# One-core hybrid attention layer: six gates into the seven-product pairs, two key sets as separate heads, named attention buffers, softmax scaling on two engines

## The chip, the cores and the metric

One core of one Trainium2 chip runs the whole layer. The metric is the device time of one execution in microseconds (us). The core's engines are TensorE (PE in the profile; PEld is its weight load), VectorE (DVE), ScalarE (ACT), GpSimd (POOL) and SyncE (SP), whose queue issues most of the transfers.

## What is computed

One decoder layer over 1024 tokens of width 1024, fp32 in and out: a norm, one wide projection, three attention mixers, a gated merge, an output projection, and a gated FFN with a short convolution.

```python
proj = h @ w_in[l] + b_in[l]
(qa, ka, va, fa, qb, kb, vb, qc, kc_, vc_, ksl, vsl, kwn, vwn, gc, gates) = jnp.split(proj, split_at, axis=-1)
y_a = fox_attention(qa, ka, va, fa)             # 4 heads, causal, decay = cumsum(log_sigmoid(fa))
y_b = dilated_attention(qb, kb, vb, dil_slopes) # 6 heads, windows 128/512/2048 at strides 1/4/16
y_c = nsa_attention(qc, kc_, vc_, ksl, vsl, kwn, vwn, gc, nsa_slopes, ...)  # 6 heads
#   per head:  o = gb[..., 0:1] * o_c + gb[..., 1:2] * o_s + gb[..., 2:3] * o_w
#   o_c: compressed keys, o_s: selected blocks of 64 keys, o_w: the last 512 keys
g = jax.nn.sigmoid(gates).reshape(B_, S, 3, D)
merged = (g[:, :, 0] * (y_a @ w_pa[l]) + g[:, :, 1] * (y_b @ w_pb[l])
          + g[:, :, 2] * (y_c @ w_pc[l]))
x = x + merged @ w_o[l]
x = x + conv_ffn(rms_norm(x, norm2_g[l]), w_up[l], conv_w[l], conv_b[l], w_down[l])
```

The 3072 columns of `gates` are 24 tiles of 128 features; a "gate" below is one of these tiles for all 1024 tokens.

## The kernel before

Every fp32 operand is split into a high and a low part (`hTh`, `hTl`; `wh`, `wl`), and a product takes three matmuls (`mm3`, L273 to L275). A 128-column weight tile against 1024 tokens is 8 x 2 x 3 = 48 matmuls of 128x512 (`dense`). In `proj_pairs` two weight tiles are taken together by a seven-product scheme (Strassen): 7 x 4 x 3 = 84 matmuls of 128x512 instead of 96, paid for with sums of weight tiles (L562 to L571) and of token tiles (`token_sums`, L461 to L474) on POOL, DVE and ACT and with adds of the products on DVE (L596, L597).

The stages, in us from the start of the span: norm and transposes to 57; `fox_decay` (L711 to L727, a chain over DVE, ACT and two small matmuls L721, L722), gates 0 and 1 (`gate`, evacuated by DVE at L1400, stored from ACT's queue at L1403), the token sums and eight tiles of `proj_vn` (L662, L694) to about 115; nine pairs to 297; key and value compression (`compress_in`, `compress`) with gate 2 to 348; attention to 832; the gates left over, and `branch`, to about 902; `merge` to 985; output projection, FFN and the last norm to 1758.

In attention the order of PE, DVE and ACT is written out beforehand by a planner, `Flow`: processes ask for an engine with a level and a cost, or for a place in a ring (`S` 2, `T` 2, `PV` 1, `dn` 1, `p` 4, `th` 3), and the lowest level that is ready goes first. One unit is two blocks of 128 queries of a head. `strips` makes the scores (L787, L790, L791); `soften` takes the maximum (L814), the exponential with its sum (ACT, L822), then on DVE the floor and reciprocal of the sum (L833, L834) and the multiply of the row (L836, or L838 where the NSA gate is a second factor); `turner` transposes blocks into one bank (L881); `splitter` makes the high part on ACT (`th`, L897) and the low part on DVE (`tl`, L900); `products` sums into the one `PV` bank (L927, L928); `pv_out` copies on ACT (L943), adds on DVE (L947) and stores 64 KB (L952) from a ring of four `yt` tiles that the planner does not know of. There are 64 units: an NSA unit holds compressed, selected and local keys in one `PV` sum. Where PE has nothing else, `fill` gives it the matmuls of gates 3 and up (L1428), evacuated by ACT (L1439) from the one `dn` bank and stored by SP (L1442).

Behind attention `gate` finishes the gates that `fill` has not reached, while `branch` loads eight 512 KB tiles of the mixers' outputs (L1477), casts them (ACT, L1478) and subtracts (DVE, L1479). `merge` needs all of `y_a`, then `y_b`, then `y_c`.

## Time and profile before

| | |
|---|---|
| median of 3 runs | 1759.94 us (1757.18 to 1762.91) |
| the profiled execution, its own time | 1759.76 us |
| span of its trace | 1758.0 us |
| TensorE busy in the span | 1676.7 us, 95% |
| VectorE, ScalarE, GpSimd busy | 74%, 44%, 27% |

The span runs from the first to the last instruction of the trace; 1.76 us lie around it. Busy shares are means over stages with different limits, so the stretches of single stages matter more than the table. "Granted clock" is the share of full speed that TensorE was given. A wait is put down to the engine and line that came last.

### The profile page before, as it was taken

What the parts mean: (1) busy time and instruction counts of PE and PEld (TensorE: products, weight loads), DVE (VectorE), ACT (ScalarE), POOL (GpSimd) and SP (SyncE); (2) the same over time, 40 slices, a digit from 0 to 9 for tenths busy, and PEclk for the clock granted to TensorE, in tenths of its full rate; (3) what the DMA queues carried; (4) which work ended last, traced back from release to release, by engine and by line L of the source; (5) the groups of instructions that cost most, each with busy time, mean ns of one, the idle gap of its engine ahead of it and who ended that gap; (6) DMA issues with size and microseconds to landing.
All of it is one profiled execution on the core that took longest, in us unless ns stands there. A gap on an engine that the chain in (4) does not pass through costs nothing.

```text
span 1758.0 us, 24330 instructions
## 1 busy us (share of the span) xinstructions
PE 1676.7 (95%) x8504; PEld 1383.7 (79%) x8504; DVE 1301.9 (74%) x2189; ACT 777.6 (44%) x1493; POOL 465.9 (27%) x326
## 2 busy tenths in 40 slices
PE   6889999899999999999999999899999999999998
PEld 6688888678787877787787788688888878888876
DVE  8856676567886888787227616999999999866764
ACT  5323443356454655565425413433333334354452
POOL 3652322100101000100214320655456554200000
PEclk9989999999999999999999999999999999999999
DMA  6445566867786235311625630144545445487661
GB/s 203 127 117 144 156 168 171 200 171 193 202 222 177 53 85 161 95 34 34 216 96 196 209 131 13 31 162 144 191 156 192 168 154 163 135 265 235 209 227 55
DMA packets 224321, 266.49 MB, mean 152 GB/s; under 512 B 20712, under 2 KB 160078, under 8 KB 223990
## 3 DMA queue, kind: packets, MB, share of 16 engines
q1 hardware_dynamic: 219862, 254.81, 48.6%
q10 hardware_dynamic: 3888, 7.34, 1.2%
q0 software_dynamic: 448, 2.78, 0.6%
q8 instruction: 67, 1.10, 0.3%
q14 instruction: 56, 0.46, 0.1%
HBM read 187.23 MB, written 80.36 MB: 152 GB/s over the span
## 4 chain that ended last, share of the span: by engine, by line
PE 57%; DVE 21%; issue 7%; DMA 5%; ACT 5%; POOL 3%; SPq 0%; POOLq 0%; DVEq 0%; ACTq 0%
PE dn L1428 8%; PE dn L273 5%; PE dn L274 5%; PE dn L275 5%; PE S L275 3%; PE S L274 3%; PE T L881 3%; PE S L273 3%; DVE t L1690 3%; DVE u L1748 3%; PE PV L928 2%; PE T L275 2%; PE T L273 2%; PE T L274 2%; PE S L791 2%
## 5 line engine op out<-in xcount | busy, mean ns | idle before, releaser
L897 ACT CAST th<-T 128x512 fp32r<-128x512 f32 (+2 forms) x202 | 100.4, 507 | 92.3 <-PE T L881 88.2
L1456 POOL TENSOR_TENSOR wl<-wr,wh 128x1024 fp32r<-128x1024 f32 x15 | 35.8, 2387 | 392.3 <-ACT wh L1452 285.7
L900 DVE TENSOR_TENSOR tl<-T,th 128x512 fp32r<-128x512 f32 (+2 forms) x202 | 115.3, 586 | 28.5 <-ACT th L897 27.2
L814 DVE TENSOR_REDUCE sm<-S 128x1 f32<-128x640 f32 (+7 forms) x128 | 88.1, 713 | 38.2 <-PE S L791 37.6
L1428 PE MATMUL dn<-hTh,wh 128*128 128x512 f32 x240 | 101.7, 424 | 10.7 <-ACT f L1439 8.1
L1690 DVE SCALAR_TENSOR_TENSOR t<-u,ccols,t 128x511 f32<-128x511 f32 (+1 forms) x88 | 95.7, 1088 | 7.5 <-ACT t L1685 6.4
L927 PE MATMUL PV<-th,v 128*128 128x256 f32 (+1 forms) x362 | 94.1, 280 | 6.6 <-DVE yt L947 5.8
L1428 PE MATMUL dn<-hTh,wl 128*128 128x512 f32 x240 | 99.7, 415 | 0.0
L1428 PE MATMUL dn<-hTl,wh 128*128 128x512 f32 x240 | 99.1, 413 | 0.0
L881 PE MATMUL T<-ident,p 128*128 128x128 f32 x610 | 97.9, 277 | 0.2 <-DVE p L838 0.2
L822 ACT ACTIVATE p<-S,sm 128x640 f32<-128x640 f32 (+7 forms) x128 | 90.9, 715 | 15.1 <-DVE sm L814 13.2
L928 PE MATMUL PV<-tl,v 128*128 128x256 f32 (+1 forms) x362 | 91.3, 286 | 4.8 <-DVE tl L900 4.6
L791 PE MATMUL S<-k,q 114*128 114x512 f32 (+6 forms) x240 | 90.1, 384 | 0.0
L251 POOL TENSOR_TENSOR wl<-wr,wh 128x384 fp32r<-128x384 f32 (+2 forms) x35 | 51.8, 1480 | 135.7 <-ACT wh L249 126.0
L787 PE MATMUL S<-k,q 128*128 128x512 f32 (+3 forms) x240 | 81.7, 340 | 1.9 <-ACT p L822 1.8
L273 PE MATMUL dn<-hTh,wh 128*128 128x512 f32 x204 | 81.1, 397 | 1.2 <-ACT f L1439 0.8
L274 PE MATMUL dn<-hTl,wh 128*128 128x512 f32 x204 | 80.7, 395 | 0.0
L928 PEld LDWEIGHTS PV<-tl,v 128*128 128x128 f32 x362 | 69.3, 191 | 12.9 <-DVE tl L900 8.2
L927 PEld LDWEIGHTS PV<-th,v 128*128 128x128 f32 x362 | 69.3, 191 | 11.8 <-DVE yt L947 7.8
L881 PEld LDWEIGHTS T<-ident,p 128*128 128x128 f32 x610 | 70.7, 141 | 5.8 <-DVE tl L900 1.2
L1615 POOL TENSOR_TENSOR su<-wr 128x512 f32<-128x512 f32 x20 | 31.6, 1579 | 143.2 <-DMA wr<-w_up 84.6
L275 PE MATMUL dn<-hTh,wl 128*128 128x512 f32 x176 | 69.4, 395 | 0.0
(784 smaller groups left out, 5377.5 us busy)
## 6 DMA issues: line engine op xcount, KB each, us to landing
wr<-w_up SPq DMA_DIRECT2D x66, 256.0 KB
wr<-w_in SPq DMA_DIRECT2D x26, 512.0 KB
gr<-dg SPq DMA_DIRECT2D x24, 512.0 KB
t<-w_down SPq DMA_DIRECT2D x22, 512.0 KB
dt<-t SPq DMA_DIRECT2D x22, 512.0 KB
wr<-dl SPq DMA_DIRECT2D x39, 256.0 KB
x<-x SPq DMA_DIRECT2D x16, 512.0 KB
dg<-f SPq DMA_DIRECT2D x30, 256.0 KB
```

The lines of the kernel that those rows point to most:

```text
L273: nc.tensor.matmul(out, st[0], mv[0], start=first, stop=False)
L274: nc.tensor.matmul(out, st[0], mv[1], start=False, stop=False)
L275: nc.tensor.matmul(out, st[1], mv[0], start=False, stop=last)
L791: nc.tensor.matmul(out, q.t[1][0:R, qs], k.t[1][0:R, cs], start=False, stop=True)
L822: nc.scalar.activation(o.rearrange("p a b -> p (a b)"), u, AF.Exp, bias=mx[:, x:x + 1], accum_out=sm[:, 2 + x:3 + x])
L881: nc.tensor.transpose(ps[:, n * P:(n + 1) * P], b(), self.ident)
L897: nc.scalar.copy(g.th[:, cs], ps[:, cs])
L900: yield "DVE", 0, 0.07 + cs.stop * 1.04e-3, lambda: nc.vector.tensor_tensor(g.tl[:, cs], ps[:, cs], g.th[:, cs].bitcast(F32), ALU.subtract)
L927: nc.tensor.matmul(unit.pv[:, oc], w, g.th[:, cs], start=first and i == 0, stop=False)
L928: nc.tensor.matmul(unit.pv[:, oc], w, g.tl[:, cs], start=False, stop=e)
L1428: nc.tensor.matmul(p, w[i][:, k], self.hT[hh][j][:, k], start=x == 0, stop=x == 23)
L1690: nc.vector.scalar_tensor_tensor(o, i, cw[2 - sh], o, ALU.mult, ALU.add)
```

## The change

- `PAIRED = 18`: gates 18 to 23 leave `fill` and `gate` and become three more pairs of `proj_pairs` (252 matmuls of 128x512 for 288). Their tiles go to `dg` from the pairs' own buffers by SP.
- The selected (`n`) and local (`w`) keys of an NSA head become separate heads: 88 units for 64, each with its own `PV` sum, copy, add and store. `dy_c` gets two planes, and `branch` loads both and adds them (L1514 to L1517): 11 loads of 512 KB instead of 8.
- Attention buffers get names that the planner hands out: PSUM `S0`, `S1`, `PV`, and `X0` to `X2` shared by transposes and `fill`; SBUF `p0` to `p5`, four `th`/`tl`, eight `y`. The planner now counts the stores and loads (`move`).
- `soften` makes the two factors on DVE (`factors`, 128x2, the NSA gates multiplied in), and each row's multiply is offered to DVE (L864) and ACT (L865); in the planned order 104 of 176 stand on DVE and 72 on ACT, these 72 with 34,432 of the 78,080 columns.
- Gates 0 and 1 are evacuated by ACT, gate 2 by DVE, and `fox_decay` moves behind `proj_vn`.

```diff
+    PAIRED = 18
+        gate = lambda f: (C_G + f * P, 20 + f, lambda side: lambda hh, src: nc.sync.dma_start(
+            self.dg[f][:, hh * 512:hh * 512 + 512], src))
-                 (k("s", C_KSL, 18, 0), k("w", C_KWN, 19, 0)))
+                 (k("s", C_KSL, 18, 0), k("w", C_KWN, 19, 0)),
+                 *((gate(f), gate(f + 1)) for f in range(self.PAIRED, 24, 2)))
...
-        self.S, self.T, self.PV, self.dn = (Ring(self, n) for n in (2, 2, 1, 1))
-        self.p, self.th, self.ce = (Ring(self, n) for n in (4, 3, 2))
+        self.S, self.PV = r("S0", "S1"), r("PV")
+        self.T = self.dn = r("X0", "X1", "X2")
+        self.p, self.th, self.y, self.ce = r(*(f"p{i}" for i in range(6))), r(*range(4)), r(*(f"y{i}" for i in range(8))), r(0, 1)
...
+        def factors():
+            nc.vector.tensor_scalar(ls, sm[:, 2:4], TINY, None, ALU.max)
+            nc.vector.reciprocal(sm[:, 6:8], ls)
+            if pair.gates is not None:
+                nc.vector.tensor_tensor(sm[:, 6:8], sm[:, 6:8], pair.gates, ALU.mult)
...
+    def norm(self, pair, x, left):
+        nc, F = self.nc, self.F
+        p, f, n = pair.blocks[x], pair.sm[:, 6 + x:7 + x], (pair.rows[x][2] - pair.rows[x][1] + 1) * P
+        yield [("DVE", 1, 0.13 + n * 0.47e-3, lambda: nc.vector.tensor_scalar(p, p, f, None, ALU.mult)),
+               ("ACT", 3, 0.16 + n * 0.85e-3, lambda: nc.scalar.mul(p, p, f))]
...
     def pv_out(self, unit):
+        place = yield F.y
...
-            if f > 2:
+            if f != 2:
                 nc.scalar.activation(gt[:, cs], ps, AF.Identity, bias=self.cols[:, 20 + f:21 + f])
+                self.step(2)
             else:
-                out = nc.vector.tensor_scalar(gt[:, cs], ps, self.cols[:, 20 + f:21 + f], None, ALU.add)
-                with self.tc.issue_after(out.ins):
-                    self.step(2)
+                nc.vector.tensor_scalar(gt[:, cs], ps, self.cols[:, 20 + f:21 + f], None, ALU.add)
...
-        for f in range(3, 21):
+        for f in range(3, self.PAIRED):
...
-            raw = pool.tile([P, S], F32, "gr")
-            nc.sync.dma_start(raw, dy[k])
+            raw, *more = (self.st.tile([P, S], F32, "gr") for _ in range(dy[k].shape[0]))
+            nc.sync.dma_start(raw, dy[k][0])
+            for x in more:
+                nc.sync.dma_start(x, dy[k][1])
+                nc.vector.tensor_tensor(raw, raw, x, ALU.add)
...
         self.proj_va()
-        self.fox_decay()
         self.gate(0)
...
         self.proj_vn(vn)
+        self.fox_decay()
...
-        self.ap2 = Pool(self, "att2", {"p": 4, "pc": 2})
+    ORDER = (("f", 0), ("d", 0), ("d", 1), ("f", 1), ("d", 2), ("d", 3), ("s", 0), ("f", 2), ("d", 4), ("d", 5),
+             ("s", 1), ("f", 3), ("w", 0), ("w", 1), ("w", 2), ("n", 0), ("n", 1), ("n", 2), ("w", 3), ("w", 4), ("w", 5),
+             ("n", 3), ("n", 4), ("n", 5))
```

The order of ACT in the early part, before: the exponential and logarithm of `fox_decay` (`fax`, `flf`, L713 and L714) stand among the casts of `proj_vn`'s weights (`bh`) and of the token sums (`T1h`).

```order
L638 CAST bh_168_814<-wr_171_821 128x548
L461 CAST T1h_120_470<-f4_148_689 128x512
L713 ACT_TABLE_LOAD
L713 ACTIVATE fax_151_698<-fax_151_698 128x32
L714 ACT_TABLE_LOAD
L714 ACTIVATE flf_152_699<-fax_151_698,cm_150_696 128x32
L638 CAST bh_168_814<-wr_172_826 128x548
L638 CAST bh_168_814<-wr_173_831 128x548
```

And in the change (L731 and L732 are `fox_decay`, L1436 is the evacuation of gate 0, `f4`):

```order
L656 CAST bh_161_786<-wr_165_798 128x548
L1436 ACTIVATE f4_150_696<-dn_157_709,cols_95_364 128x512
L656 CAST bh_161_786<-wr_166_803 128x548
L473 CAST T2h_122_472<-f4_148_689 128x512
L1440 DMA dg_60_165<-f4_150_696 128x512
L473 CAST T2h_122_472<-sh_159_774 128x512
L731 ACT_TABLE_LOAD
L731 ACTIVATE fax_204_1176<-fax_204_1176 128x32
L473 CAST T3h_124_474<-sl_160_775 128x512
L732 ACT_TABLE_LOAD
L732 ACTIVATE flf_205_1177<-fax_204_1176,cm_203_1174 128x32
```

`fox_decay` has gone behind the second half of the token sums, and ACT has the gates' evacuations between its casts.

The order of ACT in the middle of attention, before: casts `th`, exponentials (L822) and the copies of finished units.

```order
L943 COPY yt_1345_7083<-PV_1334_7026 64x256
L822 ACTIVATE p_1347_7094,sm_1336_7043<-S_1337_7044,sm_1336_7043 128x640
L897 CAST th_1348_7097<-T_1344_7078 128x512
L897 CAST th_1352_7109<-T_1350_7100 128x384
L822 ACTIVATE p_1356_7123,sm_1336_7043<-S_1346_7088,sm_1336_7043 128x768
L822 ACTIVATE p_1358_7146,sm_1354_7112<-S_1355_7113,sm_1354_7112 128x640
```

And in the change, at the like place (L841 exponential, L865 multiply of a row, L970 copy, L923 cast `th`):

```order
L923 CAST th1_1251_6813<-X2_1247_6793 128x256
L923 CAST th2_1253_6823<-X0_1250_6809 128x384
L841 ACTIVATE p3_1256_6833,sm_1243_6781<-S0_1244_6782,sm_1243_6781 128x640
L865 ACTIVATE p4_1248_6796<-p4_1248_6796,sm_1237_6751 128x384
L970 COPY y7_1259_6852<-PV_1249_6803 64x256
L841 ACTIVATE p2_1261_6860,sm_1243_6781<-S1_1255_6826,sm_1243_6781 128x640
L923 CAST th0_1264_6874<-X2_1260_6854 128x512
L970 COPY y0_1267_6887<-PV_1262_6864 64x256
```

ACT's queue has a new kind of instruction in it, the multiply L865, with an exponential before it and a copy, an exponential and a cast behind.

The order of SP's queue behind attention, before: the last gate tiles stored by `fill` (L1442), then the loads of `branch` (L1477) and of `merge` (L1489).

```order
L1442 DMA dg_60_165<-f4_1795_9118 128x512
L1477 DMA gr_1799_9161<-dy_a0_49_154 128x1024
L1477 DMA gr_1800_9165<-dy_a1_50_155 128x1024
L1477 DMA gr_1803_9171<-dy_b0_51_156 128x1024
L1442 DMA dg_60_165<-f4_1795_9118 128x512
L1477 DMA gr_1804_9175<-dy_b1_52_157 128x1024
L234 DMA wr_1814_9202<-w_in 128x8x128
L1477 DMA gr_1805_9179<-dy_b2_53_158 128x1024
L1477 DMA gr_1808_9185<-dy_c0_54_159 128x1024
L1477 DMA gr_1809_9189<-dy_c1_55_160 128x1024
L1477 DMA gr_1810_9193<-dy_c2_56_161 128x1024
L1489 DMA gr_1852_9572<-dg_60_165 128x1024
```

And in the change (L1479 gates, L1514 and L1516 the two planes, L1529 `merge`'s gate tiles):

```order
L1479 DMA dg_60_165<-f4_1896_9597 128x512 x2
L246 DMA wr_1936_9838<-w_pb 128x3x128
L1514 DMA gr_1900_9641<-dy_a0_49_154 128x1024
L1514 DMA gr_1901_9645<-dy_a1_50_155 128x1024
L1514 DMA gr_1904_9651<-dy_b0_51_156 128x1024
L1529 DMA gr_1933_9819<-dg_60_165 128x1024
L1514 DMA gr_1905_9655<-dy_b1_52_157 128x1024
L1514 DMA gr_1906_9659<-dy_b2_53_158 128x1024
L1514 DMA gr_1909_9665<-dy_c0_54_159 128x1024
L1529 DMA gr_1939_9844<-dg_60_165 128x1024
L1516 DMA gr_1910_9666<-dy_c0_54_159 128x1024
L1514 DMA gr_1911_9672<-dy_c1_55_160 128x1024
```

Both halves of the last `fill` gate are now stored ahead of the first load of `branch`, and gate tiles for `merge` stand between those loads.

## Rows read from the trace of the kernel before

**Rows 1.** Busy time, share of the span and instructions of each engine, from the profile's page.

```profile
span 1758.0 us, 24330 instructions
PE 1676.7 (95%) x8504; PEld 1383.7 (79%) x8504; DVE 1301.9 (74%) x2189; ACT 777.6 (44%) x1493; POOL 465.9 (27%) x326
```

**Rows 2.** Stretches of the program: length, each engine's busy time, granted clock, DMA.

```profile
core 0: us, PE busy (x) PEld busy (x) DVE busy (x) ACT busy (x) POOL busy (x), PEclk, DMA share, GB/s
...
57.00:118.00 61.00, 50.42 (x284) 45.07 (x285) 39.37 (x62) 17.98 (x32) 38.50 (x40) 0.89 0.47 132
...
348.40:832.00 483.60, 461.82 (x2977) 384.66 (x2978) 381.90 (x929) 274.24 (x678) 39.19 (x20) 0.99 0.49 131
832.00:902.00 70.00, 68.25 (x299) 55.49 (x299) 12.77 (x9) 26.50 (x32) 12.72 (x6) 1.00 0.49 159
```

**Rows 3.** The same view of 44 us inside the seven-product pairs.

```profile
132.00:176.00 44.00, 44.00 (x196) 36.45 (x195) 29.29 (x40) 15.98 (x26) 12.20 (x9) 1.00 0.53 143
```

**Rows 4.** TensorE's waits in attention, 348 to 832 us: total, times, longest.

```profile
PE dn L1428 <- ACT f L1439: 7.3, 11, 0.9
PE PV L927 <- DVE yt L947: 6.1, 6, 3.1
PE PV L928 <- DVE tl L900: 4.6, 5, 2.1
```

**Rows 5.** TensorE's waits before the compression, 0 to 345 us.

```profile
PE T L721 <- DVE flf L716: 5.9, 1, 5.9
PE dn L273 <- DVE f L1400: 4.7, 1, 4.7
```

**Rows 6.** Stretches of 4 us, columns as in rows 2.

```profile
64.00:68.00 4.00, 4.00 (x11) 2.98 (x9) 3.48 (x7) 0.62 (x1) 3.25 (x4) 0.50 0.76 204
...
92.00:96.00 4.00, 4.00 (x20) 4.00 (x20) 3.90 (x6) 0.93 (x2) 2.95 (x5) 0.54 0.37 116
...
416.00:420.00 4.00, 4.00 (x14) 3.21 (x14) 3.80 (x8) 1.48 (x4) 0.00 (x0) 0.57 0.58 167
```

**Rows 7.** Timeline of TensorE where the pairs begin: start, length, instruction.

```profile
114.36 0.39 PE L273 MATMUL dn<-hTh,wh 128*128 128x512 f32 x1
```

**Rows 8.** Timeline of VectorE: first and last of the token sums.

```profile
53.69 1.44 DVE L464 TENSOR_TENSOR f<-hTh,hTh 128x512 f32<-128x512 f32 x1
...
97.14 1.02 DVE L462 TENSOR_TENSOR T3l<-f,T3h 128x512 fp32r<-128x512 f32 x1 [0.33 <-ACT T3h L461]
```

**Rows 9.** Chain of waits, one piece of attention: start, length, what.

```profile
402.47 11.72 DMA dyb<-yt
```

**Rows 10.** VectorE's groups in attention, 348 to 834 us, by shape: total, mean ns.

```profile
L947 DVE TENSOR_TENSOR yt<-PV,yt 64x256 f32<-64x256 f32 x64 | 26.8, 418 | 12.2 <-ACT yt L943 11.2
...
L834 DVE RECIPROCAL sm<-sm 128x2 f32<-128x2 f32 x64 | 10.6, 166 | 2.2
...
L836 DVE TENSOR_SCALAR p<-p,sm 128x640 f32<-128x640 f32 x4 | 2.2, 554 | 0.1
```

**Rows 11.** ScalarE's groups: L943 in attention, the two casts in the whole span.

```profile
L943 ACT COPY yt<-PV 64x256 f32<-64x256 f32 x64 | 23.4, 366 | 40.9 <-PE PV L928 35.9 <-DMA dyb<-yt 3.9
...
L570 ACT CAST wh<-wr 128x512 fp32r<-128x512 f32 x24 | 14.9, 623 | 22.8 <-PE dn L275 6.2 <-POOL wr L564 5.2 <-PE T L275 4.4
...
L249 ACT CAST wh<-wr 128x1024 fp32r<-128x1024 f32 x11 | 11.5, 1047 | 11.4 <-PE dn L274 11.4
```

**Rows 12.** Timeline of TensorE: the last attention product.

```profile
831.76 0.28 PE L928 MATMUL PV<-tl,v 128*128 128x128 f32 x1
```

**Rows 13.** Timeline of SP's DMA queue behind attention.

```profile
834.40 0.88 SPq L1477 DMA_DIRECT2D gr<-dy_a  x2
...
846.18 6.84 SPq L1477 DMA_DIRECT2D gr<-dy_c  x3
```

**Rows 14.** Chain of waits behind attention.

```profile
847.30 6.47 DMA gr<-dy_c
```

**Rows 15.** Timeline of VectorE: the last subtract of the branches.

```profile
857.35 2.58 DVE L1479 TENSOR_TENSOR yl<-gr,yh 128x1024 fp32r<-128x1024 f32 x1 [1.25 <-ACT yh L1478]
```

More of the change, by code (lines that the diff above doesn't have):

```diff
@@ L181, in step @@
         elif isinstance(ask, Ring):
-            if ask.n and not ask.waiting:
-                ask.n -= 1
-                self.resume(g)
+            if ask.names and not ask.waiting:
+                self.resume(g, ask.names.pop(0))
             else:
@@ L771, in strips @@
             yield k.ready
-            yield F.S
-            yield F.p
+            bank = yield F.S
+            place = yield F.p
             def scores():
@@ L824, in soften @@
         yield "ACT", 2, 0.24 * len(n) + sum(n) * P * 0.86e-3, exponentials
-        F.S.give()
+        F.S.give(bank)
         pair.left -= 1
@@ L860, in pair_steps @@
             st = lambda grp=grp: [v.t[:, kb, :] for kb, _ in grp]
-            self.t_step(unit, [e[1] for e in grp], st, pair.done, v, (1 if pair.joint else 2) if end else 0, last and end)
+            self.t_step(unit, [e[1] for e in grp], st, pair.done, v, pair.places if end else (), last and end)
     def t_step(self, unit, ents, st, need, v, free, last):
@@ L868, in turner @@
     def turner(self):
[L869 removed]
+        nc, F = self.nc, self.F
         while True:
@@ L964, in poke @@
         while F.loads and F.loads[0][0]():
-            _, what, box = F.loads.pop(0)
+            _, what, box, kb = F.loads.pop(0)
             box.t = what()
-            F.after(8.0, lambda box=box: box.ready.set(F))
+            F.after(F.move(kb), lambda box=box: box.ready.set(F))
     def attention(self):
@@ L986, in head @@
                     out.append(self.Box(t=None, ready=Mark()))
-                    F.loads.append((cond, what, out[-1]))
+                    F.loads.append((cond, what, out[-1], {"q": 900, "k": 900, "v": 512}[kind]))
             return out
@@ L1093, in attention, with group_head @@
-        for kind, h in ORDER:
-            yield from {"f": fox_head, "d": dil_head, "s": select, "n": nsa_heads}[kind](h)
+        def group_head(kind, h):
+            g, r = divmod(h, 3)
+            q = heads[kind, h][0]
+            k, v = heads[kind, 3 * g][1:]
+            vc = self.Box(t=self.vcs[g, 0 if r == 0 else 1], ready=Mark())
+            vc.ready.on = True
+            c0 = 0 if r == 0 else (r - 1) * 64
+            for ip in range(4):
+                a, b = 2 * ip, 2 * ip + 1
+                u = self.Box(pv=None, end=(lambda: free("v")) if ip == 3 and r == 2 else None,
+                             out=(self.dy["c"][h // 2][int(kind == "w")], h % 2, slice(ip * 256, ip * 256 + 256)))
+                rows = []
+                for qi in (a, b):
+                    lo = max(qi - 4, 0) if kind == "w" else 0
+                    mk = {qi: self.mC}
+                    if kind == "w" and qi >= 4:
+                        mk[qi - 4] = self.mW
+                    rows.append((qi, lo, qi, mk))
+                p = yield from self.strips(q, k, 98 if kind == "w" else 114, rows,
+                                           gates=self.gsig[:, a:a + 2, h * 3 + 1 + (kind == "w")])
+                if kind == "n":
+                    pc, ready = pcs[g]
+                    self.t_step(u, [[(x, lambda i=i, c0=c0: pc[:, i, c0:c0 + P]) for x, i in enumerate((a, b))]],
+                                lambda vc=vc: [vc.t], ready, vc, (), False)
+                self.pair_steps(u, v, p, True)
+            free("q")
+            if r == 2:
+                free("k")
@@ L1298, in nsa_select @@
                 done = Mark()
-                F.proc(self.nsa_soften(g, r, half, ps, pc, imp, bc, before, done))
+                F.proc(self.nsa_soften(g, r, half, ps, bank, pc, imp, bc, before, done))
                 before = done
@@ L1303, in nsa_select, with nsa_soften @@
         return pc, before
-    def nsa_soften(self, g, r, half, ps, pc, imp, bc, before, done):
+    def nsa_soften(self, g, r, half, ps, bank, pc, imp, bc, before, done):
         nc, ap, F = self.nc, self.ap, self.F
@@ L1363, in nsa_rows @@
         s8 = yield "DVE", 1, 2.8, select
-        yield F.T
-        yield F.th
+        bank = yield F.T
+        place = yield F.th
         def turn():
-            pst = self.psA.tile([P, 512], F32, "T")
+            pst = self.psA.tile([P, 512], F32, bank)
             for i in range(4):
@@ L1380, in nsa_rows @@
         sr = yield "ACT", 1, 0.5, high
-        F.T.give()
+        F.T.give(bank)
         for r in range(3):
             nc.sync.dma_start(self.dax[6 + 3 * g + r][0:16, 512:1024].bitcast(F32), sr.bitcast(F32))
-        yield 3.0
-        F.th.give()
+        yield F.move(96)
+        F.th.give(place)
         F.marks.add(f"sel{g}")
```

257 lines of the change are left out of this document (121 added, 136 removed).

## The prediction

> **What bounds the kernel now.** I read the page first: TensorE is busy 1676.7 of 1758.0 us, no other engine over 74% [rows 1]. So the time is TensorE's work plus its pauses, and a change gains by removing matmuls, by removing pauses, or not at all. Then the stretches [rows 2]: inside the pairs TensorE is full, 196 matmuls in 44.00 us, 0.2245 us for one of 128x512 [rows 3]. Two of the stretches that the change touches have slack: the early part (10.6 us idle of 61) and attention (21.8 idle of 483.6). Then TensorE's waits in them. In attention three make up 18.0 us: the evacuation of `fill`'s one bank (7.3), the add that frees the one `PV` bank (6.1) and the low part of a transposed block (4.6) [rows 4]. Early, two waits make up 10.6 us: the logarithm chain of `fox_decay` (5.9) and the evacuation of gates 0 and 1 on VectorE (4.7) [rows 5]. Last the granted clock in short stretches: after such pauses it was 0.50 and 0.54 early and 0.57 in attention, with TensorE busy all 4 us [rows 6]; full is 2.4 GHz and half is 1.2 GHz, so those stretches lost 2.0, 1.8 and 1.7 us.
>
> **Matmuls.** Six gates cost 252 matmuls as pairs and 288 outright; I count 36 fewer in the two orders, all of 128x512: 36 x 0.2245 = **-8.1 us**. The three pairs also need sums of weights and adds of products on VectorE and GpSimd. In the pairs these are busy 29.3 and 12.2 of 44 us [rows 3], so three pairs more, with the same sums for each, are costed at nothing; if that cover went, they would have to take half as long again before VectorE held TensorE up. The token sums are made once and serve all pairs.
>
> **The early part.** From 57 us to the first product of the pairs at 114.36 [rows 7] TensorE waits 10.6 us [rows 5] and loses about 3.8 to the lower clock. In the change the `fox_decay` chain comes behind `proj_vn`, and the gates' evacuation goes to ScalarE, which is busy only 18.0 of 61 us. What is late next is VectorE's token sums: from 53.69 to 98.2 us [rows 8], less four evacuations that leave it, still before TensorE needs them if the pairs begin at about 104. And the two small `fox_decay` matmuls now stand right ahead of the pairs, behind a ScalarE chain in which the table loads lie among casts. Ends: 0 (the new place waits as long as the old) and -14.4. I take **-9**: the waits go, 1.6 us of them come back at the new place, and I leave the clock's share to the range. The compression keeps its work; gate 2, on VectorE before and after, is costed at zero.
>
> **Attention.** 101 fewer `fill` matmuls stand ahead of the last product (590 for 691), which is in the -8.1 or moves behind attention; it is no gain by itself. The pauses: the `fill` bank's 7.3 goes to about 1, since three banks rotate (-6.3). The `PV` bank stays single and is handed over 88 times, not 64; each costs a copy and an add, 0.37 + 0.42 us [rows 10, 11], which TensorE covers with other work: it paid 6.1 of some 50. The longest single wait belongs to the ring of four `yt`, where a store took 11.72 us to give a tile back [rows 9] and ScalarE stood 3.9 us for it [rows 11]; eight tiles, known to the planner, take that away, while 24 more handovers add about 2.3. Net -2. The low part (4.6) falls to 2, since four `th`/`tl` and three banks let transposes run further ahead of their products (-2.6). Fewer pauses leave the clock up for some 2 us more. Together **-12.9**, say -13. Ends: -20 (all 18.0 and the clock) and +18.8 (nothing saved, and all 24 extra handovers in the open, 24 x 0.78). The first end is nearer to what 64 handovers did.
>
> What the other engines pay there: on VectorE 72 of 176 multiplies leave, 0.55 us for the common 640 columns, about 36 us; 24 adds (10 us) and 48 factor products of 128x2, near the 0.17 us of the reciprocal of that size (8 us), come [rows 10]; 382 becomes about 364. On ScalarE no multiply of this form is in the trace. The nearest are casts from SBUF to SBUF, 0.623 us for 512 columns and 1.047 for 1024 [rows 11], thus 0.20 + 0.00083 a column; 72 multiplies with 34,432 columns make 42.8 us, 0.59 each. With 24 copies, 274 becomes about 325. In some 450 us neither engine is full. Six more loads of queries, 24 stores and their packets meet DMA engines that are half busy [rows 2].
>
> The Trainium skill (Perfetto Trace Analysis, Optimizing Scalar/DVE Operations) holds that work is worth offloading from VectorE to ScalarE if VectorE is saturated, and that grouping pays; here VectorE is at 79% in attention [rows 2], and splitting heads is the opposite of grouping. By that rule the attention term would be 0, and the sum 13 us higher.
>
> **Behind attention.** Before, 29 `fill` and 288 gate matmuls (71 us) cover the loading of `branch`; in the change 34 and 96 (29.2 us) do. From the last product at 831.76 [rows 12] the loads began 2.6 us later [rows 13] and the last low part was done at 859.9 [rows 15], 28.2 us behind. Now the first load stands behind both stores of the last `fill` gate, which needs its 34 matmuls first: about 6 us later. Three more loads come at 6.84/3 = 2.3 each [rows 13], and three adds like the 1.23 us of the subtract alone: 28.2 + 6 + 6.8 + 3.7 = 44.7. TensorE can go on for 29.2 plus the merge's first tile without `c`'s last third, 42 matmuls (9.4): 38.6. So 6 us open, and with `merge`'s gate loads between, **+7**. Ends: 0, and +18.7 if each extra load takes the whole 6.47 us that the chain shows for one [rows 14].
>
> **Sum.** -8.1 - 9 - 13 + 7 = -23.1: span 1734.9. The profiled execution took 1759.76, 1.76 over its span and 0.2 under the median, so 1736.7, **1737 us**. This case's own range: attention and the loads at their good ends give 1723 (-7 and -7), the early part at 0 with 4 us more of pauses in attention gives 1750.
>
> **Rivals.**
> *Attention gives nothing back* (chance 0.17). The pauses move: 88 handovers and a longer road over ScalarE eat what the banks give. For it: `PV` is still one bank. Against: `fill` is at hand at every pause. 1750 us.
> *The branch loads stall* (0.10). Every extra load is waited for in full: +18.7 for +7, so 1749 us. For it: SP's queue holds them in order behind the gate stores. Against: before, one wait of 6.47 us covered all three loads of `c` [rows 13, 14].
> *TensorE isn't the bound, so fewer matmuls give nothing* (0.07): 1737 + 8.1 = 1745 us. For it, weight loads are busy only 79% [rows 1]. Against: where TensorE does nothing but such matmuls, without a gap, weight loads show 36.45 of 44.00 us [rows 3], so some 80% is this kernel's full mark. The Trainium skill (Perfetto Trace Analysis, Identifying the Most-Contended Engine) says that matmul busy time is no good measure and weight-load busy time a better one; by that rule TensorE has a fifth to spare.
> *Slower: the multiplies stand in ScalarE's way* (0.11). ScalarE works its queue in order; a multiply of 0.59 us in front of a `th` cast delays the low part, the product, and the bank that the product frees. If all 72 delay TensorE by their own length, +42.8 comes on top: 1737 + 42.8 = 1780 us. It turns into a loss from 23.1/0.59 = 39 of the 72. For it: 24 of 88 units are new short links, and the like delay already cost 4.6 us. Against: ScalarE is idle 209 of 483.6 us [rows 2], and the planner gives a multiply to it only where it is free.
> That the change does not do what it says would be matmuls or multiplies not moved; the orders show both moved, so it gets no chance.
>
> **How the numbers follow.** The forecast has 0.55. A measurement can tell about 0.3% from no change, 5.3 us here, so faster means under 1754.7. The forecast gives nearly all of its 0.55 to faster; attention-gives-nothing, the loads and the last rival give 0.13, 0.07 and 0.06; that is 0.80 with rounding. Same gets 0.09, from their upper tails, and slower 0.11. The range, 1721 to 1758, leaves out the slower rival and the far tail of the forecast.
>
> **What would show it.** Right: TensorE's work falls by about 8 us; pairs begin near 104 us; the waits for the `fill` bank's evacuation fall to about 1 us; ScalarE's groups show 72 multiplies near 0.59 us; TensorE stands for some 7 us behind attention, waiting for the last casts of `c`. Wrong: the pairs still begin at 112 or later; waits of products for `th`, `tl` or the `PV` add sum to over 15 us; a gap over 12 us before the merge.

## The result, and the profile after

The change takes 1746.81 us (median of 4 runs, 1745.82 to 1749.2) for 1759.3 before (4 runs): ratio 0.9929, 95% interval 0.9909 to 0.9949. That is faster by 0.7%, clear of the noise and within the range; of the 22.9 us forecast some 12.5 came. The profiled executions differ by 13.9 us (1758.0 and 1744.1 us of span), and the rest of this section says where.

The page of the change, its span and engines [rows 1]:

```profile
span 1744.1 us, 24501 instructions
PE 1661.0 (95%) x8468; PEld 1379.2 (79%) x8468; DVE 1313.2 (75%) x2230; ACT 830.5 (48%) x1599; POOL 469.1 (27%) x332
```

Four marks cut both traces into stretches: the first product of the pairs [rows 7], the first matmul of `fill`, the last attention product [rows 12] and the end.

| stretch | before | change | fewer or more matmuls, at 0.2245 us | left over | forecast |
|---|---|---|---|---|---|
| to the first product of the pairs | 114.4 | 116.2 | 0 | +1.9 | -9 |
| pairs and compression | 234.0 | 285.1 | +252: +56.6 | -5.5 | 0 |
| attention | 483.4 | 455.6 | -101: -22.7 | -5.1 | -13 |
| behind attention | 926.2 | 887.2 | -187: -42.0 | +3.0 | +7 |
| sum | 1758.0 | 1744.1 | -36: -8.1 | -5.8 | -15 |

The early part, TensorE's waits from 0 to 330 us, which answer to [rows 5]:

```profile
PE dn L285 <- ACT f L1436: 9.5, 4, 5.7
PE dn L285 <- DVE tm L680: 4.6, 2, 3.5
```

And the stretches of the change that answer to [rows 2], columns as there:

```profile
57.00:118.00 61.00, 48.05 (x276) 42.51 (x275) 35.46 (x58) 19.32 (x34) 37.64 (x40) 0.92 0.45 130
...
401.30:857.10 455.80, 432.76 (x2878) 368.35 (x2878) 365.10 (x933) 319.98 (x772) 34.28 (x18) 0.98 0.54 148
```

The two waits of [rows 5] are gone, and 9.5 and 4.6 us stand in their place; the pairs begin 1.9 us later than before. ScalarE's timeline shows why the first is there:

```profile
80.56 0.62 ACT L473 CAST T3h<-f 128x512 fp32r<-128x512 f32 x1 [4.69 <-DVE f L486]
83.40 0.62 ACT L473 CAST T4h<-f 128x512 fp32r<-128x512 f32 x1 [2.22 <-POOL f L489]
83.92 0.68 ACT L1436 ACTIVATE f<-dn,cols 128x512 f32<-128x512 f32 x1
```

L1436 evacuates a gate. It stands behind two casts of token sums (L473), which wait 4.7 us for VectorE and 2.2 us for GpSimd: ScalarE takes them up in that order, so TensorE pays for sums that nobody needs yet.

In attention, TensorE's waits from 401.3 to 857.1 us, to be read beside [rows 4]:

```profile
PE S L805 <- ACT p L841: 7.1, 4, 5.3
PE X L1408 <- DVE s L1398: 4.6, 2, 2.4
PE S L809 <- DMA q<-dq_c: 2.5, 1, 2.5
PE PV L954 <- DVE tl L926: 1.8, 3, 1.1
PE X L907 <- DVE tl L926: 1.7, 1, 1.7
PE X L907 <- DVE p L864: 1.6, 1, 1.6
PE PV L953 <- DVE y L974: 1.2, 2, 0.7
PE S L809 <- DMA v<-dv_b: 1.0, 1, 1.0
PE X L907 <- ACT f L1476: 0.9, 1, 0.9
PE X L1465 <- ACT f L1476: 0.4, 1, 0.4
```

And ScalarE's one long wait for a transfer there:

```profile
ACT f L1476 <- DMA dg<-f: 12.3, 1, 12.3
```

The three waits of before have shrunk as forecast: `fill`'s bank from 7.3 to 0.4 us (and 0.9 for transposes in the shared banks), the `PV` add from 6.1 to 1.2 with 88 handovers, the low part from 4.6 to 1.8. But TensorE's idle time in attention went from 21.8 to 23.1 us, since other waits are new: 4.6 us for the NSA selection (`s`), 2.5 and 1.0 for loads, 1.7 and 1.6 of transposes for a bank and for a multiplied row. And the largest, 7.1 us for an exponential, is as long as the longest of before. ScalarE's timeline at that place:

```profile
584.70 1.03 ACT L1489 CAST wh<-wr 128x1024 fp32r<-128x1024 f32 x1
598.03 0.69 ACT L1476 ACTIVATE f<-X,cols 128x512 f32<-128x512 f32 x1 [12.30 <-DMA dg<-f]
598.62 0.36 ACT L841 ACTIVATE p<-S,sm 128x128 f32<-128x128 f32 x1
```

The chain of waits there, start, length and what:

```profile
584.92 13.01 DMA dg<-f
```

And three stretches of 4 us, columns as in [rows 2]:

```profile
592.00:596.00 4.00, 1.53 (x8) 0.96 (x8) 2.19 (x9) 0.00 (x0) 0.00 (x0) 1.00 0.70 190
596.00:600.00 4.00, 0.42 (x1) 0.42 (x2) 0.37 (x3) 1.97 (x7) 0.00 (x0) 0.81 0.13 33
600.00:604.00 4.00, 4.00 (x14) 3.07 (x13) 2.46 (x7) 2.74 (x8) 0.00 (x0) 0.50 0.50 4
```

An evacuation of `fill` (L1476) waits 12.3 us in ScalarE's queue until the store of the gate before it has landed; that store took 13.0 us, behind 15 loads issued since 573 us; its issue alone held SP's queue for 6.2 us. Exponentials stand behind it, TensorE runs dry, and the next 4 us go at half clock (0.50, the 1.2 GHz level). The reason is in the pools. Before, the "stage" pool held two `f4` tiles; the "att" pool that takes its place names none, and so has one. The planner counts neither. I had read that the pools were merged and not what that did to `f4`. Counted in steps of 4 us as idle plus what the lower clock cost, the pauses of attention came to 27.7 us before and 32.2 in the change.

Behind attention, SP's queue, to be read beside [rows 13]:

```profile
860.31 6.48 SPq L1479 DMA_DIRECT2D dg<-f  x2
...
868.83 0.90 SPq L1514 DMA_DIRECT2D gr<-dy_a  x2
```

The first load of `branch` is issued 12 us behind the last product (856.9), not the 8.6 that I had assumed; but TensorE waits there only 4.7 us for evacuations and casts, from 857 to 930 us:

```profile
PE dn L285 <- ACT f L1436: 3.4, 1, 3.4
PE dn L285 <- ACT yh L1518: 1.3, 1, 1.3
```

### The profile page after: what moved, and what is told of

Its sections match the earlier page's. It is cut to its first block, busy times and chain, and to the rows that moved or that the text cites. A ratio compares the mean times of both kernels' runs of the same rounds, so it can differ in the third digit from the quotient of the medians.

```text
span 1744.1 us, 24501 instructions
## 1 busy us (share of the span) xinstructions
PE 1661.0 (95%) x8468; PEld 1379.2 (79%) x8468; DVE 1313.2 (75%) x2230; ACT 830.5 (48%) x1599; POOL 469.1 (27%) x332
## 4 chain that ended last, share of the span: by engine, by line
PE 57%; DVE 20%; DMA 7%; issue 6%; ACT 5%; POOL 4%; SPq 0%; POOLq 0%; DVEq 0%; ACTq 0%
PE X L1465 6%; PE dn L287 5%; PE dn L285 5%; PE dn L286 5%; PE S L286 4%; PE S L287 4%; PE S L285 4%; PE X L907 3%; PE T L287 3%; DVE t L1730 3%; PE T L286 3%; PE T L285 3%; PE PV L954 2%; PE S L809 2%; DVE u L1788 2%
## 5 line engine op out<-in xcount | busy, mean ns | idle before, releaser
L926 DVE TENSOR_TENSOR tl<-X,th 128x512 fp32r<-128x512 f32 (+2 forms) x202 | 116.5, 586 | 24.9 <-ACT th L923 22.9
L923 ACT CAST th<-X 128x512 fp32r<-128x512 f32 (+2 forms) x202 | 101.1, 507 | 39.6 <-PE X L907 36.0
L907 PE MATMUL X<-ident,p 128*128 128x128 f32 x610 | 99.4, 278 | 4.4 <-DVE tl L926 1.7
L841 ACT ACTIVATE p<-S,sm 128x640 f32<-128x640 f32 (+7 forms) x128 | 90.9, 715 | 16.6 <-DVE sm L833 15.9
L809 PE MATMUL S<-k,q 98*128 98x128 f32 (+6 forms) x240 | 91.7, 390 | 3.5 <-DMA q<-dq_c 2.5
L805 PE MATMUL S<-k,q 128*128 128x512 f32 (+2 forms) x240 | 83.0, 346 | 7.1 <-ACT p L841 7.1
L1465 PE MATMUL X<-hTh,wl 128*128 128x512 f32 x208 | 86.5, 416 | 0.0
L1465 PE MATMUL X<-hTl,wh 128*128 128x512 f32 x208 | 86.3, 415 | 0.0
L1465 PE MATMUL X<-hTh,wh 128*128 128x512 f32 x208 | 85.5, 411 | 0.4 <-ACT f L1476 0.4
L907 PEld LDWEIGHTS X<-ident,p 128*128 128x128 f32 x610 | 70.9, 142 | 13.9 <-DVE tl L926 3.2
L285 PE MATMUL dn<-hTh,wh 128*128 128x512 f32 x148 | 60.0, 405 | 10.2 <-ACT f L1436 10.2
```

Of the source, the lines that this page charges most:

```text
L285: nc.tensor.matmul(out, st[0], mv[0], start=first, stop=False)
L809: nc.tensor.matmul(out, q.t[1][0:R, qs], k.t[1][0:R, cs], start=False, stop=True)
L841: nc.scalar.activation(o.rearrange("p a b -> p (a b)"), u, AF.Exp, bias=mx[:, x:x + 1], accum_out=sm[:, 2 + x:3 + x])
L907: nc.tensor.transpose(ps[:, n * P:(n + 1) * P], b(), self.ident)
L923: nc.scalar.copy(g.th[:, cs], ps[:, cs])
L926: yield "DVE", 0, 0.07 + cs.stop * 1.04e-3, lambda: nc.vector.tensor_tensor(g.tl[:, cs], ps[:, cs], g.th[:, cs].bitcast(F32), ALU.subtract)
```

## The experiments

Twelve kernels ran. Ratios are to runs of the kernel before on the same chip; the change itself has 0.9929 (0.9909 to 0.9949). "Pairs begin" and "attention" (first `fill` matmul to last product) are in us, from the profile of one execution each; that of e3 took 1746.26 us, 7 over the median of its five, and that of e9 1753.21, 3 over.

| run | edit | median, us | ratio, 95% interval | pairs begin | attention |
|---|---|---|---|---|---|
| e1 | early part undone | 1748.41 | 0.9920 (0.9900 to 0.9941) | 114.6 | 454.9 |
| e2 | gates 0, 1 on VectorE, `fox_decay` late | 1739.26 | 0.9872 (0.9854 to 0.9889) | 115.2 | 449.2 |
| e3 | casts tied behind ScalarE's evacuations | 1739.32 | 0.9874 (0.9855 to 0.9894) | 110.4 | 456.3 |
| e4 | two `f4`, four `y` | 1741.18 | 0.9879 (0.9864 to 0.9894) | 116.2 | 447.9 |
| e5 | e3 and e4 | 1732.53 | 0.9824 (0.9811 to 0.9838) | 108.8 | 450.0 |
| e6 | e5, all multiplies on VectorE | 1739.04 | 0.9853 (0.9829 to 0.9877) | 109.3 | 456.8 |
| e7 | e5, no gate pairs | 1751.07 | 0.9932 (0.9919 to 0.9945) | 110.6 | 450.6 |
| e8 | e5, `fill` with a bank of its own | 1731.85 | 0.9817 (0.9799 to 0.9836) | 109.3 | 448.0 |
| e9 | e5, gate pairs first | 1750.17 | 0.9928 (0.9908 to 0.9949) | 109.3 | 454.9 |
| e10 | e5, joint NSA heads | 1731.69 | 0.9827 (0.9804 to 0.9851) | 109.2 | 472.1 |
| e11 | e5, later weights of the dilated heads | 1721.63 | 0.9773 (0.9748 to 0.9798) | 110.8 | 439.3 |
| e12 | e11, `fill` stored from ScalarE | 1720.50 | 0.9765 (0.9742 to 0.9789) | 111.0 | 435.1 |

### The early part: e1, e2, e3

```diff
-            if f != 2:
-                nc.scalar.activation(gt[:, cs], ps, AF.Identity, bias=self.cols[:, 20 + f:21 + f])
-                self.step(2)
+            if f > 2:
+                nc.scalar.activation(gt[:, cs], ps, AF.Identity, bias=self.cols[:, 20 + f:21 + f])
             else:
-                nc.vector.tensor_scalar(gt[:, cs], ps, self.cols[:, 20 + f:21 + f], None, ALU.add)
+                out = nc.vector.tensor_scalar(gt[:, cs], ps, self.cols[:, 20 + f:21 + f], None, ALU.add)
+                with self.tc.issue_after(out.ins):
+                    self.step(2)
```

That is e2; e1 has it too, and `fox_decay` back between `proj_va` and `gate(0)`. e3 keeps ScalarE and ties the order there:

```diff
-                nc.scalar.activation(gt[:, cs], ps, AF.Identity, bias=self.cols[:, 20 + f:21 + f])
-                self.step(2)
+                out = nc.scalar.activation(gt[:, cs], ps, AF.Identity, bias=self.cols[:, 20 + f:21 + f])
+                with self.tc.issue_after(out.ins):
+                    self.step(2)
```

> The change with its early part undone: gates 0 and 1 evacuated by VectorE again, with the next token sums queued behind the evacuation, and fox_decay ahead of gate 0. Theory (the early part of the change gained nothing, it moved two waits into a ScalarE queue): the pairs begin at 114.4 us as before instead of 116.2, and the time falls by 1 to 3 us against the change (1744 to 1746). Rival (the early part did gain its 9 us, and something else in the stage took it): the time rises by 5 to 9 us (1752 to 1756).

> The change with only the evacuation of gates 0 and 1 put back on VectorE; fox_decay stays behind proj_vn. Theory (ScalarE's queue is what holds gates 0 and 1 up, the move of fox_decay is good): the waits for gate evacuations on ScalarE (9.5 us) go, a VectorE wait of 4 to 8 us stands in their place, the pairs begin at 108 to 112 us and the time falls by 4 to 8 us against the change. Rival (VectorE's token sums bound the stage whatever evacuates the gates): the pairs begin at 114 or later and the time is within 2 us of the change.

> The change with the gates still evacuated by ScalarE, but the next token sums' casts on ScalarE tied behind each evacuation. Theory (casts that wait for VectorE and GpSimd stand ahead of the evacuations in ScalarE's queue): the 9.5 us of waits for the evacuation shrink to under 3 us, the pairs begin at 105 to 111 us, and the time falls by 5 to 10 us. Rival (the token sums themselves are late): the wait turns up at the adds of proj_vn, and the pairs begin within 2 us of 116.2.

Measured: e1 is the change again (0.9920), its pairs begin at 114.6 us. So the early part as a whole gained nothing that can be told. In e2 the pairs begin at 115.2: there the theory missed (108 to 112) and the rival was right, while the time fell by 0.0057 or 10 us, which is neither the rival's 2 us nor to be had from the early part. Two rows of TensorE's timeline in e2, in front of `proj_vn`'s tiles:

```profile
82.05 0.57 PE L285 MATMUL dn<-bh,hTh 128*128 128x274 f32 x1 [7.00 <-DVE f L1438]
...
90.96 0.60 PE L285 MATMUL dn<-bh,hTh 128*128 128x274 f32 x1 [4.10 <-DVE f L1438]
```

With `fox_decay` out of the way the evacuations of gate 1 come 7.0 and 4.1 us late on VectorE (4.67 before): the wait moved from one place in that queue to another, as the token sums take VectorE's time either way. In e3 they begin at 110.4, 5.9 us earlier than in the change; TensorE's waits for ScalarE's evacuations fall from 9.5 to 7.4 us and the one for `tm` from 4.6 to 0.8. TensorE's timeline in e3:

```profile
72.94 0.79 PE L285 MATMUL dn<-hTh,wh 128*128 128x512 f32 x1 [3.86 <-ACT f L1436]
...
82.60 0.39 PE L285 MATMUL dn<-bh,hTh 128*128 128x274 f32 x1 [2.42 <-ACT f L1436]
...
91.28 0.40 PE L285 MATMUL dn<-bh,hTh 128*128 128x274 f32 x1 [0.79 <-DVE tm L680]
```

The start of the pairs is at the late end of what I expected and the waits miss it (under 3 us), since the casts of an earlier step still stand ahead; the time, 0.0055 or 9.7 us under the change, is at the good end of 5 to 10. e2's gain lies in attention, which is 6.4 us shorter than the change's though nothing in it was edited and the `f4` wait is still there (12.9 us). Counted as above, its pauses there are 25.7 us for 32.2, about half of that in the clock. Why an edit of the early part does this is open, and it is a warning: a gain of 0.005 in time does not by itself show its cause.

### One `f4` tile: e4 and e5

```diff
-        self.p, self.th, self.y, self.ce = r(*(f"p{i}" for i in range(6))), r(*range(4)), r(*(f"y{i}" for i in range(8))), r(0, 1)
+        self.p, self.th, self.y, self.ce = r(*(f"p{i}" for i in range(6))), r(*range(4)), r(*(f"y{i}" for i in range(4))), r(0, 1)
...
-                                               "pc": 2})
+                                               "pc": 2, "f4": 2})
```

> The change with two f4 tiles in the attention pool, as the pool before had, instead of one; the 4 KB come from the y ring (four tiles instead of eight). Theory (one f4 tile lets an evacuation wait 12.3 us in ScalarE's queue for the store of the gate before, and this stops TensorE at 588 to 604 us and at half clock behind it): that wait goes, and the time falls by 6 to 11 us against the change (1736 to 1741). Rival (the stop is the NSA selection's, and would be there anyway): TensorE still stands some 8 us there, and the time is within 2 us of the change. If the y ring of eight was what helped, waits of copies for a store come back and eat a part.

Measured: the wait of the evacuation is gone from ScalarE, the pauses of attention fall from 32.2 to 22.1 us, attention is 7.7 us shorter and the ratio 0.9879: 0.0050 under the change, 8.8 us of 1760, as expected. With e2 in mind it is the trace, and the same step from e3 to e5 (0.0050), that put this down to the tile. Four `y` tiles, with the planner counting their stores, bring no wait for a store back; so eight were not what helped.

> The change with two f4 tiles (four y tiles) and with the next token sums' casts tied behind each gate evacuation on ScalarE, the edits of the third and fourth run together. Theory (two separate losses, 5 to 6 us early and about 8 us in attention): the gains add up, 12 to 15 us below the change, ratio to before 0.984 to 0.986. Rival (what is won early is lost again later, in the pairs or the compression, as the third run's profile hints): no more than 9 us below the change, ratio 0.988.

Measured: 0.9824, 0.0105 under the change, or 18 us; that is what e3 and e4 have together (0.0055 and 0.0050), so the rival falls. But one wait of 7 us stands in attention again, at nearly the same place, now by way of VectorE (e4 has it too). VectorE's timeline in e5:

```profile
595.53 0.18 DVE L1183 TENSOR_TENSOR amx<-ln 128x16 f32<-128x16 f32 x1 [5.19 <-DMA ln<-dlse]
597.95 0.17 DVE L1184 TENSOR_TENSOR amx<-amx,ln 128x16 f32<-128x16 f32 x1 [2.24 <-DMA ln<-dlse]
```

And TensorE's, a little later:

```profile
600.55 0.58 PE L954 MATMUL PV<-tl,v 128*128 128x256 f32 x1 [6.97 <-DVE tl L926]
```

These are the small loads of `dil_merge` (the weights by which the dilated heads are merged). In the change VectorE shows no wait for them: it came to them late itself, behind ScalarE. With `f4` mended it comes too early. The planner allows 12 us for them.

### The dilated heads' weights and the gate stores: e11, e12

```diff
-        yield 12.0
+        yield 24.0
```
```diff
-        yield 0.1
-        nc.sync.dma_start(self.dg[f][:, cs], gt[:, cs])
+        nc.scalar.dma_start(self.dg[f][:, cs], gt[:, cs])
```

The first alone is e11 (in `dil_merge`, behind its loads), both are e12 (the second in `gate_out`).

> The kernel with both mended, with the planner allowing 24 us instead of 12 for the small loads that the merge of the dilated heads waits for. Theory (VectorE stood 7.4 us in its queue for these loads at 590 to 598 us, and TensorE 7.0 us behind it): this wait goes, 5 to 9 us of the time with it. Rival (another wait takes its place, since the plan has only to be shifted): within 2 us.

> As the run with the late weights, and the gates of fill are stored from ScalarE's queue, right behind their evacuation, instead of from SP's, where the last two hold the loads of branch back. Theory: the first load of branch is issued 5 to 7 us earlier, TensorE's waits behind attention (5 us for ScalarE's casts) go, and the time falls by 2 to 6 us against the run with the late weights. Rival (issuing from ScalarE's queue delays what stands behind it there): no gain, or a loss of up to 5 us.

Measured: e11 has 0.9773, 0.0051 or 9 us under e5; VectorE waits for no transfer in attention any more, and the pauses there are 13.8 us, for 24.6 in e5. e12 has 0.9765, not to be told from e11. SP's queue in e12:

```profile
843.17 0.39 SPq L246 DMA_DIRECT2D wr<-w_pb  x1
843.66 1.45 SPq L1514 DMA_DIRECT2D gr<-dy_a  x2
```

The gate store no longer holds the queue, and yet the first load of `branch` goes out 10.4 us behind the last product, as in e11 (845.6, with the last product at 835.2): a weight load (L246) stands ahead of it and waits 8.2 us in SP's queue until GpSimd is done with its tile. The rival was nearer. Both are the fastest kernels here.

### Where the scaling runs: e6

```diff
-        yield [("DVE", 1, 0.13 + n * 0.47e-3, lambda: nc.vector.tensor_scalar(p, p, f, None, ALU.mult)),
-               ("ACT", 3, 0.16 + n * 0.85e-3, lambda: nc.scalar.mul(p, p, f))]
+        yield "DVE", 1, 0.13 + n * 0.47e-3, lambda: nc.vector.tensor_scalar(p, p, f, None, ALU.mult)
```

> The kernel with both mended, and every row's multiply on VectorE, so 72 multiplies (48 to 50 us measured on ScalarE) become some 37 us on VectorE. Theory (the split matters little, since neither engine is full): within 4 us of the kernel with both mended. Rival one (VectorE is the nearer bound, the split is what saved the waits for low parts): waits of products and transposes for low parts rise by 8 us or more, and the time by 5 to 12 us. Rival two (the slower case of the prediction: multiplies stand in ScalarE's way): the time falls by 3 us or more.

Measured: 0.9853 for 0.9824, 5 us slower, with intervals that just overlap; the slower case of the prediction is out, since taking the multiplies off ScalarE does not help. The 5 us may be too low: e6's shifted plan has no wait for the dilated heads' weights, as e5 has, and against e11, where that wait is mended, it is 14 us slower. No run changes the split alone in a plan without that wait. Rival one has the size but not the sign by which I meant to know it: TensorE's waits for low parts are 5.7 us here and 10.8 in e5, 7.0 of them the one above. The planned order shows another way: with VectorE slower the plan fits 643 `fill` matmuls ahead of the last product instead of 597, and fewer are left to cover the loads behind (5.8 us of waits for the casts, 2.8 in e5); this accounts for 3 of the 5 us. The price of one multiply is in ScalarE's groups of the change, by shape (total, mean ns):

```profile
L865 ACT ACTIVATE p<-p,sm 128x640 f32<-128x640 f32 x15 | 12.3, 830 | 2.6 <-DVE sm L853 2.5
L865 ACT ACTIVATE p<-p,sm 128x1024 f32<-128x1024 f32 x7 | 8.2, 1168 | 0.0
```

All 72 take 50.0 us, 0.69 each, where I had estimated 42.8 from the casts [rows 11].

### The three gate pairs: e7 and e9

e7 sets `PAIRED = 24`. e9 moves the pairs of gates:

```diff
-        pairs = ((q("a", C_QA, 0, 0), q("a", C_QA + P, 1, 2)), (k("a", C_KA, 2, 0), k("a", C_KA + P, 3, 2)),
+        pairs = (*((gate(f), gate(f + 1)) for f in range(self.PAIRED, 24, 2)), (q("a", C_QA, 0, 0), q("a", C_QA + P, 1, 2)), (k("a", C_KA, 2, 0), k("a", C_KA + P, 3, 2)),
...
-                 (k("s", C_KSL, 18, 0), k("w", C_KWN, 19, 0)),
-                 *((gate(f), gate(f + 1)) for f in range(self.PAIRED, 24, 2)))
+                 (k("s", C_KSL, 18, 0), k("w", C_KWN, 19, 0)))
```

> The kernel with both mended, without the three pairs of gates: 36 matmuls of 128x512 more, 288 gate matmuls back behind attention. Theory (TensorE bounds; a matmul costs 0.2245 us): 8.1 us for the matmuls, less the 3 us that TensorE stood behind attention, since the branch loads are covered again: 4 to 8 us slower than the kernel with both mended. Rival (TensorE has headroom and fewer matmuls give nothing): within 2 us, or faster because the pairs' sums go.

> The kernel with both mended, with the three gate pairs at the head of the list of pairs instead of at its end; the same matmuls. Theory (besides 36 matmuls, the gate pairs at the end cover the load and split of the compression's weights, which without them cost 8.4 us of waits and a lower clock): TensorE waits 6 to 9 us more for the casts of the compression, the granted clock of that stage falls under 0.95, and the time rises by 6 to 14 us. Rival (the seven-product pairs save more than their matmuls elsewhere, wherever they stand): within 3 us of the kernel with both mended.

Measured: without the pairs 0.9932, with them at the head of the list 0.9928, at its end 0.9824. The place is worth 18 us. TensorE's longest wait in e7 from 100 us to the start of `fill`:

```profile
PE S L285 <- ACT k L1271: 8.4, 2, 7.3
```

The two longest in e9:

```profile
PE S L285 <- ACT k L1270: 9.7, 2, 7.4
PE X L1465 <- DVE vcs L1305: 2.1, 1, 2.1
```

And three stretches of e9 around the first of them, columns as in [rows 2]:

```profile
361.00:365.00 4.00, 0.00 (x0) 0.00 (x0) 2.50 (x4) 1.63 (x4) 0.57 (x3) 0.88 0.97 232
365.00:369.00 4.00, 0.63 (x2) 0.64 (x3) 0.65 (x1) 1.04 (x1) 0.00 (x0) 0.50 1.13 233
369.00:373.00 4.00, 4.00 (x15) 3.52 (x15) 1.80 (x2) 1.04 (x1) 0.00 (x0) 0.50 0.48 134
```

Where the list ends with key projections, TensorE stands for the compression's weights (8.4 and 9.7 us) and then runs at 0.50. SP's queue shows why. In e7, whose pairs end at 287.3 us:

```profile
296.89 5.28 SPq L246 DMA_DIRECT2D wr<-w_in  x2
302.26 0.53 SPq L1263 DMA_DIRECT2D cw<-cmp_k_w  x1
302.85 2.74 SPq L1270 DMA_DIRECT2D q<-cmp_k_w  x4
```

And in e5, whose pairs end at 342.9:

```profile
340.20 0.38 SPq L246 DMA_DIRECT2D wr<-w_in  x1
...
345.64 0.38 SPq L246 DMA_DIRECT2D wr<-w_in  x1
346.13 0.52 SPq L1263 DMA_DIRECT2D cw<-cmp_k_w  x1
346.69 3.20 SPq L1270 DMA_DIRECT2D q<-cmp_k_w  x4
```

The compression's weights (L1270) are not loaded during the pairs in either. Behind the pairs come some 66 matmuls of dense tiles, 15 us of work that needs none of them. With gate pairs last the loads go out 3.8 us into it; with key projections last, 15.5 us into it (in e9 too), when it is over. Ahead of them in the queue stand the last pairs' stores, which in e7 go on until 296.8, and two loads of `w_in`, the second of which waits 4.2 us more for GpSimd. These two go out 9.6 and 14.5 us behind the pairs in e7, and 2.7 us ahead of their end and 2.7 behind it in e5. So what the place of the gates buys is a queue that is free earlier. The kernel before, with key projections last too, issued its first two loads of the compression's weights at 290.5, ahead of the end of its pairs (293.0), and has no such wait: the 18 us are what the place is worth in the new kernel, not a gain of the change over before.

Counted in steps of 4 us from the pairs to the end of attention, pauses and lower clock cost 29.9 us in e5, 44.0 in e7 and 53.1 in e9. So e9 has 8.1 us less work than e7 and 9.1 us more pauses, which is why the same time comes out. Its attention is 4.9 us longer than e5's, with the same order: 1.0 us more idle and 4.0 more lost to the lower clock; why the clock fell more often there is open.

### The shared banks and the heads: e8, e10

e8 is one line; e10 has the unit of the kernel before, with both key sets in one `PV` sum, written for the new rings, and 64 units.

```diff
-        self.T = self.dn = r("X0", "X1", "X2")
+        self.T, self.dn = r("X0", "X1"), r("X2")
```
```diff
-             ("s", 1), ("f", 3), ("w", 0), ("w", 1), ("w", 2), ("n", 0), ("n", 1), ("n", 2), ("w", 3), ("w", 4), ("w", 5),
-             ("n", 3), ("n", 4), ("n", 5))
+             ("s", 1), ("f", 3), ("n", 0), ("n", 1))
...
+            (ks, kw, vs, vw), qs = heads["n", g]
```

> The kernel with both mended, with the three X banks split up as before: two for transposes, one for the gates of fill. Theory (the shared banks took the 7.3 us that TensorE waited for the evacuation of fill's one bank): 5 to 7 us of these waits come back, and the time rises by 4 to 8 us. Rival (the planner hides them as well with other work, the saving came from elsewhere): the time stays within 2 us.

> The kernel with both mended, with selected and local keys of an NSA head in one unit again: 64 units, 64 handovers of the PV bank, one plane of dy_c, 8 loads behind attention, 6 loads of queries fewer. The planner then fits all 720 fill matmuls ahead of the last product, and none is left to cover the loads of branch. Theory (the split of the heads costs little by itself and buys shorter units): the time rises, by 3 to 12 us, since TensorE stands 15 to 25 us behind attention for 8 loads and its waits for low parts in the long units grow. Rival (the split only adds 24 copies, adds and stores): the time falls by 3 us or more.

Measured: e8 0.9817 for 0.9824. The waits for `fill`'s bank come back, a little less than expected, TensorE's waits from 398 us on:

```profile
PE X L1466 <- ACT f L1477: 4.7, 6, 1.3
PE X L907 <- DVE tl L926: 4.6, 5, 1.5
PE X L907 <- DVE p L864: 2.9, 2, 1.5
```

4.7 us, for none in e5's list, and the time does not care, since e5's single wait of 7.0 us is not there. That is one stall for another; whether the shared banks would show in e11, no run tells. e10 is level with e5 too (0.9827): attention is 22 us longer with 123 more `fill` matmuls in it (27.6 us), and TensorE stands 6.5 us for the casts behind it, less than the 15 to 25 I expected. But it too lacks e5's wait of 7.0 us (its longest for a low part is 1.8), and against e11, which has split heads and not that wait either, it is 0.0054 or 9.5 us slower. So the tie with e5 does not show that splitting the heads is worth nothing; joint heads with e11's edit would, and no run has them.

## Why the prediction held, and where it did not

The direction and the range were right; most terms were not, and their errors went both ways. The time lies 10 us above the 1737 forecast, nearer to the 1745, 1749 and 1750 us of three rivals. The early part gained nothing, and attention's pauses rose by 4.5 us where I had them fall by 13, so that much of the rival "attention gives nothing back" came true, though by a store and not by the handovers that it names. What stood in for these two terms, 5.5 us in pairs and compression and 9.6 us of work in attention, was in no sum. That the total still came out at half of the forecast, inside the range, is in part luck. Of the three signs of being wrong one came: the pairs begin at 116.2 us, behind 112.

**Matmuls, -8.1.** As forecast: the counts are in the table, and e9 against e7 shows the 8.1 us as work that pauses ate. The rival by which fewer matmuls give nothing, with the Trainium skill's rule behind it (Perfetto Trace Analysis, Identifying the Most-Contended Engine), is not needed: TensorE's weight loads are at 79% in both traces, and the time followed work plus pauses. The price of 0.2245 us was too low in attention, as shown below.

**The early part, -9: came out +1.9.** The failed step is "the waits go". I had looked at how busy ScalarE is (18.0 of 61 us), not at what stands in its queue ahead of the evacuation. e3 got 5.9 us of it by order alone, e5 7.4.

**Pairs and compression, 0: came out -5.5.** The failed step is "the compression keeps its work" and costs the same: I asked what the three pairs cost and not what waits behind them. Idle and lower clock in this stretch fell from 11.2 to 5.7 us. One wait that went is the 2.1 us of `fill`'s first matmul for the compressed values, which the kernels with key projections last have (before, e7, e9); the lower clock of 1.8 us went too. For the rest no run singles out a cause: the stall of e7 and e9 was not there before.

**Attention, -13: came out -5.1.** The three waits fell by 14.6 us in place of the 11 I had summed (by 12.0, if the 0.9 and 1.7 us that transposes now wait for the shared banks are taken off), so these steps held. The step that failed is that nothing would come in their place: the store that holds the one `f4`, 8 us by e4, and behind it, hidden by it, the loads of `dil_merge`, 9 us by e11. So the pauses rose, from 27.7 to 32.2 us; with both gone they are 13.8, 13.9 fewer than before. The -5.1 come from work. In TensorE's timelines, each matmul counted from its start to the next one's, without idle and with half-clock stretches halved, the `fill` matmuls of attention took 176.2 us before and 148.1 in the change, 0.25 us each and not the 0.2245 of the pairs. So the 101 that left took 28.1 us with them, where the table has 22.7, and the step "no gain by itself" was wrong by 5.4. The other matmuls of the stretch took 279.2 us before, 275.3 in the change, and 275.6 to 277.9 in e4 to e12, whichever banks, heads or scaling they have; where these 4 us come from is open.

**ScalarE's multiplies.** Their price came out 17% above the estimate, and the slower rival is refuted by e6. The Trainium skill (Perfetto Trace Analysis, Optimizing Scalar/DVE Operations) names a saturated engine as the condition both for offloading and for grouping; VectorE was at 79% of attention before. e6 puts the gain of offloading at 5 us, give or take as much, and lacks a wait that e5 has; if the gain is one, it came without saturation.

**Behind attention, +7: came out +3.0.** The loads start even later than assumed (12 us, not 8.6), and the last low part of `c` is done 47.0 us behind the last product, not 44.7. TensorE's cover had the size assumed (130 `fill` and gate matmuls and 41 of the merge, for 42), but it lasted 44.4 us, not 38.6, since 3.4 us of waiting for an evacuation and a stretch at the lower clock lie in it. Only 1.3 us of waiting for the casts were left.

## What to carry to other kernels

When pools are merged or renamed, count the tiles of every tag before and after, and not only of those that the change speaks of: a ring that goes from two to one shows first as an engine that waits in its queue for a store. An engine's idle share does not say that work moved to it is free; read what stands ahead of that work in its queue, and what that waits for. Work with no successor in the next stage, like the gates here, can be worth putting last in a stage: the queue that issues the next stage's loads is then not held by the last stores, and here they went out 3.8 us behind the stage, not 15.5. And an edit that shifts a plan can remove a stall that it does not speak of, as e6, e8 and e10 did with e5's; such a comparison says little until both sides are free of it.
